# An encoder layer on one core: token tile 0 runs further ahead at the part boundaries, and the stationary operands move to the weights' byte

## The chip, the core and the metric

The kernel runs on one core of a Trainium2 chip. The metric is the device time of one execution in microseconds. Before the change it is 1952.46 us, the median of three runs (1952.25 to 1954.24).

## What is computed

One layer of an encoder on x of 256 tokens by 2,048 features in float32. It has three parts, each with an RMS norm before and after, and shift, scale and gate from a modulation vector (c times `w_ada`):

```python
h = modulate(rms_norm(x, ffn1_pre_g), sh1, sc1)
x = x + 0.5 * g1 * rms_norm((silu(h @ w_gate) * (h @ w_up)) @ w_down, ffn1_post_g)

h = modulate(rms_norm(x, mix_pre_g), sh2, sc2)
q, k, v, c_val, c_gate = split(h @ w_in)
attn = three dilated window attentions of rope(q), rope(k), v, combined
u = silu(layer_norm(depthwise_conv31(c_val * sigmoid(c_gate)) + conv_b))
merged = concat(rms_norm(attn), rms_norm(u)) @ w_out
x = x + g2 * rms_norm(merged, mix_post_g)

h = modulate(rms_norm(x, ffn2_pre_g), sh3, sc3)
x = x + 0.5 * g3 * rms_norm((silu(h @ w_gate) * (h @ w_up)) @ w_down, ffn2_post_g)
```

The inner width of both feed-forward parts is 5,632.

## The kernel before

**Products.** Each product of two float32 matrices is done as three TensorE products of a hi and a lo half. The 256 tokens are two token tiles, t0 and t1, of 128. Weights come in chunks of two k-tiles (2 x 128 rows by 512 columns, 512 KB): SyncE's queue loads a chunk into one of seven `raw` buffers, ScalarE casts it to `hi` (L290), and VectorE makes `lo` = raw - hi (L291); `hi` and `lo` have four buffers each (`HILO`). For each k-tile and token tile there are three matmuls: hi x xh (L316), lo x xh (L317), hi x xl (L318). The activations, 128 x 128, are the stationary operand; the weights, 128 x 512, move. There are 2,560 such triples, 7,680 matmuls.

`in_step` (L320) takes a list of chunks: it loads and casts them all, then runs all of t0's products on them, then all of t1's. `group` (L329) makes one step of each chunk, but joins the first `head` chunks, and the last `tail` chunks, into one step.

**Parts.** The first feed-forward part (ffn1) runs its first products in four stages over the features, while VectorE forms the modulation sums (L191) that the next stage needs. Then come mixing (w_in in column groups c0 to c3 for the convolution and q, k, v for the heads, then attention, convolution, and w_out as groups oa, ob, oc), and ffn2, again in stages. Work beside the products (modulation, attention, convolution) runs in lanes, which advance at a set rate at each `tick` of a chunk.

**Boundaries.** Between two parts the new x must be complete for a token tile before its norm. `next_norm` (L409) does it: `post_rstd` makes the post-norm's factor from the squares of f (POOL's power), `post_add` adds f to x in four pieces (VectorE, L405) with their squares (ScalarE, L339), and `pre_norm` scales x to `xn` (VectorE, L368), transposes it (TensorE, L371), applies the modulation (ScalarE, L376) and splits it to h (L357, L358), the stationary operand of the next part. So that t0 can go through this while TensorE still works for t1, the last group of ffn1 and the group oc3 have `TAIL` = 4 chunks in one step, all of t0 first; and the next part begins with `HEAD` = 4 chunks of c0, or g0 and u0 (four chunks) in `begin2` (L568), t0 first again.

**Addresses.** As built, the buffers of the weights (`raw`, `hi`, `lo`) begin at byte 64 of a 256-byte line. The slots of the activations (`slot`, L249: tags h and a) begin at byte 0, but for the slot `al5`, which follows a slot of `SLOT` = 1,144 elements and begins at byte 224. 128 of the 7,680 matmuls have their stationary operand there, all of them L318.

**The order of instructions** on each engine is set by a scheduler that works from dependencies and priorities, within the order of the program.

Of the kernel before, what the change touches and what calls it, by code (L numbers as in the profile page):

```python
# [34 lines left out]

HEAD = 4
TAIL = 4  # L40
# [20 lines left out]
def encoder_layer(ctx, tc, a, consts, out):  # L61
# [215 lines left out]
            return self.lo[k // 4][:, k % 4:k % 4 + n, :]  # L277


    def wchunk(w, r0, kt, cols, name):  # L280
# [12 lines left out]

    class Group:
# [6 lines left out]
            self.first, self.last, self.kx = first, last, kx  # L301
            self.chunks = -(-nk // CH)

        def load(self, c):
            kt = min(CH, self.nk - c * CH)
            return wchunk(self.w, (self.k0 + c * CH) * P, kt, self.cols, f"{self.name}_{c}")

        def products(self, c, t, hl):
            ts = slice(t * P, (t + 1) * P)
# [10 lines left out]
    def in_step(work):  # L320

        hls = [g.load(c) for g, c in work]
# [6 lines left out]
    def group(*args, head=0, tail=0, **kw):  # L329

        g = Group(*args, **kw)
        head = min(head, g.chunks - tail)
        mid = range(head, g.chunks - tail)
        for cs in (range(head), *([c] for c in mid), range(g.chunks - tail, g.chunks)):
            in_step([(g, c) for c in cs])
# [63 lines left out]
    def post_add(f, r, i, t):  # L399


        sx = small(f"sx{i}_{t}", 4)
        for db in range(4):
            xs = x[:, t, db * BLK:(db + 1) * BLK]
            nc.vector.scalar_tensor_tensor(xs, f[db][:, t, :], r, xs, op0=ALU.mult, op1=ALU.add)  # L405
            square_sum(xs, sx[:, db:db + 1], "jx")
        return rstd_parts(sx, D, f"r{i}_{t}", keep_in="rx")

    def next_norm(f, ssp, A, B, j1, i):  # L409

# [9 lines left out]
        return hT, rs  # L420
# [29 lines left out]
    def ffn_down(f, aT, wd, ba, bb, th, G, ssp, i):  # L450
        for db in range(4):
            pd = mm_ps(f"pd{i}_{th}_{db}")
            group(pd, aT, wd, ba * 4, (bb - ba) * 4, db * BLK, f"d{i}_{th}_{db}",
                  tail=TAIL if th == 1 and db == 3 else 0)
            for t in range(NT):
# [106 lines left out]
    rs = [rstd_parts(sx[t], D, f"r0_{t}", act=True, keep_in="rx") for t in range(NT)]  # L562
    for _ in first:
        pass
    hT = Parts("h1", "h", range(4))
    pre_norm(hT, rs, A1, B1, *STAGES1[0], "1_0")

    def begin2(open_group, run, order):  # L568

        gs, k1 = {}, STAGES2[0][1]  # L570
        for w, b in order[:2]:
            ps = mm_ps(f"p{w}2_{b}_0")
            gs[w, b] = open_group(w, b, 0, 0, k1, ps)
# [299 lines left out]
    drain(conv_entry)  # L873
    drain(mods)
    r2 = rc["conv"]
    for db in range(4):
        po = mm_ps(f"pc{db}")
        group(po, mT, w_out, 8, 8, db * BLK, f"oc{db}", kx=8, tail=TAIL if db == 3 else 0)
        for t in range(NT):
            nc.vector.scalar_tensor_tensor(f[db][:, t, :], po[t], r2[:, t:t + 1],  # L880
                                           f[db][:, t, :], op0=ALU.mult, op1=ALU.add)
            post_block(f, ssp, G2, t, db)


    hT, rs = next_norm(f, ssp, A3, B3, STAGES2[0][1], 3)
# [66 lines left out]
```

## Time and profile before

| | |
|---|---|
| median of three runs | 1952.46 us |
| profiled execution | 1953.91 us |
| its span | 1952.1 us |
| mean granted TensorE clock | 0.989 |
| TensorE (PE) busy | 1872.6 us, 96% |
| VectorE (DVE) busy | 1474.1 us, 76% |
| ScalarE (ACT) busy | 928.3 us, 48% |
| POOL busy | 66.0 us, 3% |
| moved by DMA | 496.29 MB, mean 254 GB/s |

The shares are means over a span with many stages; what bounds a stage has to be read in that stage. Busy times of matmuls are modelled at their ends, so the pace of TensorE is read from the starts of matmuls that follow each other. The page's part 4 follows the work that ended last back to the start.

### The profile page before, as it was taken

Reading aid. Unit: us, or ns where it says so; the run is one execution under the profiler, and the core shown is the slowest. Engines: PE = TensorE matmul, PEld = TensorE weight load, DVE = VectorE, ACT = ScalarE, POOL = GpSimd, SP = SyncE. Lnnn points to the kernel's source line nnn. Section 1 sums busy time; section 2 is a strip of 40 time slices with the busy share of each in tenths; the row PEclk is TensorE's granted clock in tenths of the full one; section 3 lists DMA queues with packets and bytes.
Section 4 is the critical chain, followed back from the end, with each engine's and each line's share of the span. In section 5 each row is a group of like instructions: output and inputs, shape, how many; then the busy total and the mean of one; then the engine's idle time right before and its main releaser. Section 6 shows DMA issues by size and latency. Waiting matters only on the chain.

```text
span 1952.1 us, 23783 instructions
## 1 busy us (share of the span) xinstructions
PE 1872.6 (96%) x8358; PEld 1527.1 (78%) x8358; DVE 1474.1 (76%) x1824; ACT 928.3 (48%) x1428; POOL 66.0 (3%) x99
## 2 busy tenths in 40 slices
PE   2999999999999999899999988999999999999997
PEld 1888877888888888688888776687888888888886
DVE  6789999787777776689997777897786556545455
ACT  3554355444444444644456655534444443444442
POOL 2000000000000000000100000000000000000000
PEclk9999999999999999899999999999999999999999
DMA  9989978999999898357555767897777777666653
GB/s 344 310 297 311 323 253 283 348 340 328 314 321 316 317 318 292 109 184 224 173 165 161 239 214 258 301 341 254 226 247 244 244 253 248 195 185 191 206 191 101
DMA packets 250392, 496.29 MB, mean 254 GB/s; under 512 B 17209, under 2 KB 42625, under 8 KB 250272
## 3 DMA queue, kind: packets, MB, share of 16 engines
q1 hardware_dynamic: 247888, 491.38, 76.1%
q0 software_dynamic: 2208, 3.32, 0.5%
q8 instruction: 65, 1.06, 0.2%
q14 instruction: 55, 0.45, 0.1%
q10 hardware_dynamic: 176, 0.07, 0.0%
HBM read 492.58 MB, written 2.12 MB: 253 GB/s over the span
## 4 chain that ended last, share of the span: by engine, by line
PE 88%; DVE 5%; DMA 3%; ACT 2%; issue 2%; POOL 0%; DVEq 0%; POOLq 0%; ACTq 0%; SPq 0%
PE pd_t L318 8%; PE pd_t L317 8%; PE pd_t L316 8%; PE pg_t L317 8%; PE pg_t L318 8%; PE pg_t L316 8%; PE pu_t L318 8%; PE pu_t L317 8%; PE pu_t L316 7%; PE pc_t L316 2%; PE pc_t L318 2%; PE pc_t L317 2%; DVE acc L191 2%; DMA ada<-in_w_ada 1%; PE pa L384 1%
## 5 line engine op out<-in xcount | busy, mean ns | idle before, releaser
L191 DVE SCALAR_TENSOR_TENSOR acc<-ada,cact,acc 128x512 f32<-128x512 f32 (+2 forms) x448 | 384.9, 897 | 12.8 <-DMA acc<-in_b_ada 8.4
L291 DVE TENSOR_TENSOR lo_d<-raw_d,hi_d 128x1024 fp32r<-128x1024 f32 x176 | 215.3, 1225 | 157.6 <-ACT hi_d L290 156.9
L290 ACT CAST hi_d<-raw_d 128x1024 fp32r<-128x1024 f32 x176 | 185.2, 1052 | 261.2 <-PE pd_t L318 181.5
L290 ACT CAST hi_g<-raw_g 128x1024 fp32r<-128x1024 f32 x176 | 185.0, 1052 | 247.2 <-PE pg_t L318 121.0
L291 DVE TENSOR_TENSOR lo_g<-raw_g,hi_g 128x1024 fp32r<-128x1024 f32 x176 | 214.4, 1222 | 105.0 <-ACT hi_g L290 104.8
L291 DVE TENSOR_TENSOR lo_u<-raw_u,hi_u 128x1024 fp32r<-128x1024 f32 x176 | 213.9, 1222 | 104.7 <-ACT hi_u L290 104.4
L290 ACT CAST hi_u<-raw_u 128x1024 fp32r<-128x1024 f32 x176 | 184.8, 1052 | 214.0 <-PE pu_t L318 94.5
L318 PE MATMUL pd_t<-hi_d,a_0l 128*128 128x512 f32 x384 | 151.2, 394 | 0.0
L317 PE MATMUL pd_t<-lo_d,a_0h 128*128 128x512 f32 x384 | 150.5, 392 | 0.0
L316 PE MATMUL pd_t<-hi_d,a_0h 128*128 128x512 f32 x384 | 150.4, 392 | 0.0
L316 PE MATMUL pg_t<-hi_g,h3h 128*128 128x512 f32 x352 | 140.4, 401 | 5.3 <-ACT hi_g L290 4.2
L316 PE MATMUL pu_t<-hi_u,h3h 128*128 128x512 f32 x352 | 139.8, 400 | 2.9 <-ACT hi_u L290 2.9
L317 PE MATMUL pu_t<-lo_u,h3h 128*128 128x512 f32 x352 | 140.0, 398 | 1.7 <-DVE lo_u L291 1.6
L317 PE MATMUL pg_t<-lo_g,h3h 128*128 128x512 f32 x352 | 139.4, 396 | 1.7 <-DVE lo_g L291 1.7
L316 PE MATMUL pg_t<-hi_g,h1h 128*128 128x512 f32 x352 | 139.4, 398 | 1.0 <-ACT hi_g L290 1.0
L318 PE MATMUL pu_t<-hi_u,h3l 128*128 128x512 f32 x352 | 139.7, 397 | 0.0
L317 PE MATMUL pg_t<-lo_g,h1h 128*128 128x512 f32 x352 | 138.7, 394 | 0.8 <-DVE lo_g L291 0.8
L318 PE MATMUL pg_t<-hi_g,h3l 128*128 128x512 f32 x352 | 139.3, 396 | 0.0
L316 PE MATMUL pu_t<-hi_u,h1h 128*128 128x512 f32 x352 | 138.8, 396 | 0.0
L318 PE MATMUL pu_t<-hi_u,h1l 128*128 128x512 f32 x352 | 138.6, 394 | 0.0
L318 PE MATMUL pg_t<-hi_g,h1l 128*128 128x512 f32 x352 | 138.6, 395 | 0.0
L317 PE MATMUL pu_t<-lo_u,h1h 128*128 128x512 f32 x352 | 137.8, 392 | 0.1
(259 smaller groups left out, 3572.1 us busy)
## 6 DMA issues: line engine op xcount, KB each, us to landing
ada<-in_w_ada SPq DMA_DIRECT2D x288, 512.0 KB, 5.3
raw_g<-in_ffn_w_gate SPq DMA_DIRECT2D x176, 512.0 KB, 4.7
raw_u<-in_ffn_w_up SPq DMA_DIRECT2D x176, 512.0 KB, 4.7
raw_d<-in_ffn_w_down SPq DMA_DIRECT2D x176, 512.0 KB, 5.7
raw_c<-in_w_in SPq DMA_DIRECT2D x64, 256.0 KB, 3.1
raw_q<-in_w_in SPq DMA_DIRECT2D x16, 512.0 KB, 4.4
raw_k<-in_w_in SPq DMA_DIRECT2D x16, 512.0 KB, 4.5
raw_v<-in_w_in SPq DMA_DIRECT2D x16, 512.0 KB, 4.2
```

The source lines that it names most:

```text
L191: tc.keep_in_program_order(nc.vector.scalar_tensor_tensor(acc, w[:, j, :], cact[:, j0 + j:j0 + j + 1], acc, op0=ALU.mult, op1=ALU.add))
L290: nc.scalar.copy(h, r)
L291: nc.vector.tensor_tensor(l, r, f32(h), op=ALU.subtract)
L316: nc.tensor.matmul(o, xh, h, start=self.first and k == 0, stop=False)
L317: nc.tensor.matmul(o, xh, l, start=False, stop=False)
L318: nc.tensor.matmul(o, xl, h, start=False, stop=self.last and k == self.nk - 1)
L384: nc.tensor.transpose(ps[:, jj * S + t * P:jj * S + (t + 1) * P], src[:, t, jj * P:(jj + 1) * P], ident)
```

## The change

**Boundaries.** The tail of each feed-forward part's last group is seven chunks (`TAIL1`), three of them with hi and lo in slots that are free by then (`TAIL_AT1`). oc2 and oc3 go together in one step of eight chunks (`TAIL_AT2`). All eight chunks of c0 have t0 first (`HEAD1`), and the first four are loaded and cast ahead of `next_norm`, into free slots of a (`HEAD_AT1`). ffn2 begins with g0, u0 and g1, six chunks, the first four again ahead (`HEAD_AT2`). `next_norm` takes the last group's evictions as a function: t0's first, t1's only behind t0's first transposes; t1's own norm comes after all of t0's. `begin2` reports six chunks instead of four, so the modulation's lane of that stage runs at 24/16 instead of 24/18 steps a chunk.

**Addresses.** `SLOT` is rounded up to 1,152 elements, so that no slot is off its line; and a tile `gap` of 64 bytes is put ahead of the first h tile. As built, all 7,680 matmuls then have both operands at byte 64.

The core of the diff:

```diff
-HEAD = 4
-TAIL = 4
+TAIL1 = 7
+TAIL_AT1 = (("hh2", "hl2"), ("hh3", "hl3"), ("gs", "ac"))
+HEAD1 = 8
+HEAD_AT1 = (("ah0", "al0"), ("ah1", "al1"), ("ah2", "al2"), ("ah3", "al3"))
+HEAD_AT2 = TAIL_AT2 = (("ah0", "ah1"), ("ah2", "ah3"), ("al2", "al3"), ("ah5", "al5"))
...
-SLOT = 4 * (S + 2 * PAD)
+SLOT = -(-4 * (S + 2 * PAD) // 64) * 64
...
-        hi = wpool.tile([P, CH, BLK], F32R, tag="hi", name=f"hi_{name}")
-        lo = wpool.tile([P, CH, BLK], F32R, tag="lo", name=f"lo_{name}")
+        if at is None:
+            hi = wpool.tile([P, CH, BLK], F32R, tag="hi", name=f"hi_{name}")
+            lo = wpool.tile([P, CH, BLK], F32R, tag="lo", name=f"lo_{name}")
+        else:
+            hi = slot(at[0], [P, CH, BLK], f"hi_{name}", F32R)
+            lo = slot(at[1], [P, CH, BLK], f"lo_{name}", F32R)
...
-    def next_norm(f, ssp, A, B, j1, i):
...
-        hT = Parts(f"h{i}", "h", range(4))
-        jh = min(HEAD * CH, j1)
+    def next_norm(hT, f, ssp, A, B, j1, i, evict):
...
+        evict(0)
         rs = [post_add(f, post_rstd(ssp, i, 0), i, 0)]
         pre_norm(hT, rs, A, B, 0, JF, i, 0, 1)
+        evict(1)
         rs.append(post_add(f, post_rstd(ssp, i, 1), i, 1))
-        pre_norm(hT, rs, A, B, JF, jh, i, 0, 1)
-        pre_norm(hT, rs, A, B, 0, jh, i, 1, 2)
-        pre_norm(hT, rs, A, B, jh, j1, i)
+        pre_norm(hT, rs, A, B, JF, j1, i, 0, 1)
+        pre_norm(hT, rs, A, B, 0, j1, i, 1, 2)
...
-                  tail=TAIL if th == 1 and db == 3 else 0)
+                  tail=TAIL1 if th == 1 and db == 3 else 0, places=TAIL_AT1)
...
+    nc.vector.memset(work.tile([P, 16], F32, name="gap"), 0.0)
     hT = Parts("h1", "h", range(4))
...
-        in_step([(g, c) for g in gs.values() for c in range(g.chunks)])
-        return {k: (g.ps, k1) for k, g in gs.items()}, k1
+        in_step(ahead2, hls=hls2 + load_all(ahead2[4:]))
+        return {k: (g.ps, STAGES2[0][1]) for k, g in heads2.items()}, len(ahead2)
...
+    c0 = Group(ps_c0, hT, a["w_in"], 0, NK, (3 * AW, 3 * AW + CW), "c0")
+    ahead = [(c0, c) for c in range(HEAD1)]
+    hls = load_all(ahead[:4], HEAD_AT1)
+    rs = next_norm(hT, f, ssp, A2, B2, NK, 2, evict)
+    in_step(ahead, hls=hls + load_all(ahead[4:]))
...
+    both = [conv_group(db) for db in (2, 3)]
+    in_step([(g, c) for g in both for c in range(g.chunks)], TAIL_AT2)
...
+    for w, b in (("g", 0), ("u", 0), ("g", 1)):
...
+    ahead2 = [(g, c) for g in heads2.values() for c in range(g.chunks)]
+    hls2 = load_all(ahead2[:4], HEAD_AT2)
+    rs = next_norm(hT, f, ssp, A3, B3, STAGES2[0][1], 3, evict)
```

How the order moves, at two places. First VectorE at the boundary from ffn1 to mixing, from t0's third addition to x (L405 before, L418 now) up to its first `xn`. L459 (now L472) evicts t1's last product, L390 multiplies it by the gate, `lo_c0_n` is a cast of chunk n of c0, `s_` are sums for the norms. Before:

```order
L405 SCALAR_TENSOR_TENSOR x_87<-f1_2_2759,pr2_0_6500,x_87 128x512
L459 TENSOR_TENSOR f1_3_2760<-pd1_1_3_t1_6302,f1_3_2760 128x512
L405 SCALAR_TENSOR_TENSOR x_87<-f1_3_2760,pr2_0_6500,x_87 128x512
L291 TENSOR_TENSOR lo_c0_1_6736<-raw_c0_1_6734,hi_c0_1_6735 128x1024
L390 TENSOR_TENSOR f1_3_2760<-f1_3_2760,G1l_5607 128x512
L291 TENSOR_TENSOR lo_c0_2_6743<-raw_c0_2_6741,hi_c0_2_6742 128x1024
L291 TENSOR_TENSOR lo_c0_3_6750<-raw_c0_3_6748,hi_c0_3_6749 128x1024
L350 TENSOR_REDUCE s_r2_0_6517<-sx2_0_6504 128x1
L350 TENSOR_REDUCE s_pr2_1_6542<-ssp1_2761 128x1
L351 TENSOR_SCALAR s_r2_0_6517<-s_r2_0_6517 128x1
L351 TENSOR_SCALAR s_pr2_1_6542<-s_pr2_1_6542 128x1
L368 TENSOR_SCALAR xn2_0_0_6523<-x_87,r2_0_6518 128x256
```

and now:

```order
L418 SCALAR_TENSOR_TENSOR x_87<-f1_2_2761,pr2_0_6528,x_87 128x512
L300 TENSOR_TENSOR lo_c0_2_6511<-raw_c0_2_6509,hi_c0_2_6510 128x1024
L418 SCALAR_TENSOR_TENSOR x_87<-f1_3_2762,pr2_0_6528,x_87 128x512
L300 TENSOR_TENSOR lo_c0_4_6739<-raw_c0_4_6737,hi_c0_4_6738 128x1024
L300 TENSOR_TENSOR lo_c0_3_6518<-raw_c0_3_6516,hi_c0_3_6517 128x1024
L472 TENSOR_TENSOR f1_3_2762<-pd1_1_3_t1_6304,f1_3_2762 128x512
L363 TENSOR_REDUCE s_r2_0_6545<-sx2_0_6532 128x1
L300 TENSOR_TENSOR lo_c0_5_6746<-raw_c0_5_6744,hi_c0_5_6745 128x1024
L364 TENSOR_SCALAR s_r2_0_6545<-s_r2_0_6545 128x1
L300 TENSOR_TENSOR lo_c0_6_6753<-raw_c0_6_6751,hi_c0_6_6752 128x1024
L381 TENSOR_SCALAR xn2_0_0_6551<-x_87,r2_0_6546 128x256
```

Casts of chunks 4 to 6 have come in, the multiply by the gate and t1's sums have moved behind `xn`.

Second, TensorE at the boundary from mixing to ffn2, where t1's first transposes (`pst3_0_1`, L371, now L384) stand among t0's products of the head. Before, in the head's third chunk (`pu2_0_0`):

```order
L317 MATMUL pu2_0_0_t0_9829<-lo_u2_0_0_0_0_9845,h3h0_9721 128x512
L318 MATMUL pu2_0_0_t0_9829<-hi_u2_0_0_0_0_9844,h3l0_9722 128x512
L316 MATMUL pu2_0_0_t0_9829<-hi_u2_0_0_0_0_9844,h3h0_9721 128x512
L317 MATMUL pu2_0_0_t0_9829<-lo_u2_0_0_0_0_9845,h3h0_9721 128x512
L371 MATMUL pst3_0_1_9795<-ident_75,xn3_0_1_9796 128x128 x2
L371 MATMUL pst3_2_1_9805<-ident_75,xn3_2_1_9806 128x128 x2
L318 MATMUL pu2_0_0_t0_9829<-hi_u2_0_0_0_0_9844,h3l0_9722 128x512
```

and now, in its sixth and last chunk (`pg2_1_0`):

```order
L325 MATMUL pg2_1_0_t0_9743<-hi_g2_1_0_0_0_9884,h3h0_9731 128x512
L326 MATMUL pg2_1_0_t0_9743<-lo_g2_1_0_0_0_9885,h3h0_9731 128x512
L327 MATMUL pg2_1_0_t0_9743<-hi_g2_1_0_0_0_9884,h3l0_9732 128x512
L325 MATMUL pg2_1_0_t0_9743<-hi_g2_1_0_0_1_9890,h3h0_9731 128x512
L384 MATMUL pst3_0_1_9851<-ident_75,xn3_0_1_9852 128x128 x2
L384 MATMUL pst3_2_1_9861<-ident_75,xn3_2_1_9862 128x128 x2
L326 MATMUL pg2_1_0_t0_9743<-lo_g2_1_0_0_1_9891,h3h0_9731 128x512
```

t1's transposes stand 14 of t0's products later (31 instead of 17 matmuls into the head).

## Rows read from the trace of the kernel before

**Rows 1.** The page, parts 1, 4 and 6, of the whole span.

```profile
PE 1872.6 (96%) x8358; PEld 1527.1 (78%) x8358; DVE 1474.1 (76%) x1824; ACT 928.3 (48%) x1428; POOL 66.0 (3%) x99
...
PE 88%; DVE 5%; DMA 3%; ACT 2%; issue 2%; POOL 0%; DVEq 0%; POOLq 0%; ACTq 0%; SPq 0%
...
raw_c<-in_w_in SPq DMA_DIRECT2D x64, 256.0 KB, 3.1
```

**Rows 2.** Stretches: us; busy PE, PEld, DVE, ACT, POOL; PE clock; DMA share; GB/s.

```profile
107.00:320.00 213.00, 210.81 (x956) 171.27 (x955) 202.58 (x257) 103.94 (x161) 4.80 (x7) 1.00 0.87 292
345.00:460.00 115.00, 115.00 (x511) 94.22 (x510) 89.57 (x76) 53.06 (x82) 2.87 (x4) 1.00 0.95 345
```

**Rows 3.** Waits of TensorE: waiting instruction, releaser, us in all, count, longest.

```profile
PE pst L371 <- DVE xn L368: 14.8, 2, 7.5
```

**Rows 4.** Timeline of VectorE, first boundary: start, us, instruction, [idle before, releaser].

```profile
793.98 0.69 DVE L459 TENSOR_TENSOR f<-pd_t,f 128x512 f32<-128x512 f32 x1 [3.23 <-PE pd_t L318]
...
805.44 0.15 DVE L350 TENSOR_REDUCE s_r<-sx 128x1 f32<-128x4 f32 x1
...
806.43 0.63 DVE L368 TENSOR_SCALAR xn<-x,r 128x256 f32<-128x256 f32 x2 [0.59 <-POOL r L352]
```

**Rows 5.** Timeline of TensorE at the same boundary.

```profile
799.10 0.40 PE L318 MATMUL pd_t<-hi_d,a_1l 128*128 128x512 f32 x1
806.84 1.12 PE L371 MATMUL pst<-ident,xn 128*128 128x128 f32 x4 [7.35 <-DVE xn L368]
```

**Rows 6.** The page, part 5: the casts (busy, mean ns, idle before).

```profile
L291 DVE TENSOR_TENSOR lo_d<-raw_d,hi_d 128x1024 fp32r<-128x1024 f32 x176 | 215.3, 1225 | 157.6 <-ACT hi_d L290 156.9
L290 ACT CAST hi_d<-raw_d 128x1024 fp32r<-128x1024 f32 x176 | 185.2, 1052 | 261.2 <-PE pd_t L318 181.5
```

**Rows 7.** Timelines of VectorE and TensorE at the second boundary.

```profile
1161.08 0.75 DVE L880 SCALAR_TENSOR_TENSOR fm<-pc_t,rcc,fm 128x512 f32<-128x512 f32 x1 [1.99 <-PE pc_t L318]
...
1173.62 0.63 DVE L368 TENSOR_SCALAR xn<-x,r 128x256 f32<-128x256 f32 x2 [0.59 <-POOL r L352]
...
1166.14 0.39 PE L318 MATMUL pc_t<-hi_oc,ml 128*128 128x512 f32 x1
1174.03 1.12 PE L371 MATMUL pst<-ident,xn 128*128 128x128 f32 x4 [7.50 <-DVE xn L368]
```

**Rows 8.** Stretches at the two boundaries, columns as in rows 2.

```profile
803.00:815.00 12.00, 7.04 (x20) 5.15 (x21) 8.00 (x21) 8.14 (x26) 1.76 (x3) 0.50 0.43 132
1163.00:1190.00 27.00, 18.39 (x73) 14.33 (x72) 19.17 (x38) 18.96 (x40) 3.09 (x4) 0.81 0.28 81
1190.00:1260.00 70.00, 63.57 (x266) 48.91 (x265) 59.80 (x93) 36.93 (x70) 3.88 (x6) 0.95 0.96 334
```

**Rows 9.** Timelines of VectorE and TensorE at the end.

```profile
1939.76 2.74 DVE L896 SCALAR_TENSOR_TENSOR f<-f,pr,x 128x512 f32<-128x512 f32 x4 [0.68 <-POOL pr L352]
1942.42 0.68 DVE L459 TENSOR_TENSOR f<-pd_t,f 128x512 f32<-128x512 f32 x1
...
1941.77 0.40 PE L318 MATMUL pd_t<-hi_d,a_1l 128*128 128x512 f32 x1
```

**Rows 10.** Timeline of TensorE: byte 224, byte 0, byte 0 early, one stationary operand.

```profile
712.25 0.40 PE L316 MATMUL pd_t<-hi_d,a_1h 128*128 128x512 f32 x1
...
715.75 0.40 PE L316 MATMUL pd_t<-hi_d,a_1h 128*128 128x512 f32 x1
...
716.45 0.39 PE L316 MATMUL pd_t<-hi_d,a_1h 128*128 128x512 f32 x1
...
725.37 0.39 PE L316 MATMUL pd_t<-hi_d,a_1h 128*128 128x512 f32 x1
...
101.60 0.40 PE L316 MATMUL pg_t<-hi_g,h1h 128*128 128x512 f32 x1
...
103.70 0.40 PE L316 MATMUL pg_t<-hi_g,h1h 128*128 128x512 f32 x1
...
1059.50 3.62 PE L761 MATMUL psmu<-co,ones 128*128 128x256 f32 x16
```

More of the change, by code (lines that the diff above doesn't have):

```diff
@@ L277, in l, with wchunk @@
             return self.lo[k // 4][:, k % 4:k % 4 + n, :]
-    def wchunk(w, r0, kt, cols, name):
+    def wchunk(w, r0, kt, cols, name, at=None):
         raw = wpool.tile([P, CH, BLK], F32, tag="raw", bufs=RAW, name=f"raw_{name}")
-        hi = wpool.tile([P, CH, BLK], F32R, tag="hi", name=f"hi_{name}")
-        lo = wpool.tile([P, CH, BLK], F32R, tag="lo", name=f"lo_{name}")
+        if at is None:
[4 more added lines that the diff above has]
+            lo = slot(at[1], [P, CH, BLK], f"lo_{name}", F32R)
         r, h, l = raw[:, :kt, :], hi[:, :kt, :], lo[:, :kt, :]
@@ L302, in __init__, with load @@
             self.chunks = -(-nk // CH)
-        def load(self, c):
+        def load(self, c, at=None):
             kt = min(CH, self.nk - c * CH)
-            return wchunk(self.w, (self.k0 + c * CH) * P, kt, self.cols, f"{self.name}_{c}")
+            return wchunk(self.w, (self.k0 + c * CH) * P, kt, self.cols, f"{self.name}_{c}", at)
         def products(self, c, t, hl):
@@ L318, in products, with load_all, in_step @@
                 nc.tensor.matmul(o, xl, h, start=False, stop=self.last and k == self.nk - 1)
-    def in_step(work):
-        hls = [g.load(c) for g, c in work]
+    def load_all(work, places=()):
+        return [g.load(c, places[n] if n < len(places) else None) for n, (g, c) in enumerate(work)]
+    def in_step(work, places=(), hls=None):
+        if hls is None:
+            hls = load_all(work, places)
         for t in range(NT):
@@ L327, in in_step, with group @@
             tick()
-    def group(*args, head=0, tail=0, **kw):
+    def group(*args, tail=0, places=(), **kw):
         g = Group(*args, **kw)
[L332 to L335, printed above, removed]
+        for c in range(g.chunks - tail):
+            in_step([(g, c)])
+        if tail:
+            in_step([(g, c) for c in range(g.chunks - tail, g.chunks)], places)
     def square_sum(src, dst, name):
@@ L407, in post_add @@
         return rstd_parts(sx, D, f"r{i}_{t}", keep_in="rx")
[L409 to L413 removed]
+    def next_norm(hT, f, ssp, A, B, j1, i, evict):
+        evict(0)
         rs = [post_add(f, post_rstd(ssp, i, 0), i, 0)]
         pre_norm(hT, rs, A, B, 0, JF, i, 0, 1)
+        evict(1)
         rs.append(post_add(f, post_rstd(ssp, i, 1), i, 1))
[L417 to L420 removed]
+        pre_norm(hT, rs, A, B, JF, j1, i, 0, 1)
+        pre_norm(hT, rs, A, B, 0, j1, i, 1, 2)
+        return rs
     def act_out(aT, i, gs, pu, name):
@@ L453, in ffn_down, with evict @@
             group(pd, aT, wd, ba * 4, (bb - ba) * 4, db * BLK, f"d{i}_{th}_{db}",
-                  tail=TAIL if th == 1 and db == 3 else 0)
-            for t in range(NT):
+                  tail=TAIL1 if th == 1 and db == 3 else 0, places=TAIL_AT1)
+            def evict(t, db=db, pd=pd):
                 if th == 0:
@@ L459, in ffn_down @@
                     nc.vector.tensor_tensor(f[db][:, t, :], pd[t], f[db][:, t, :], op=ALU.add)
-                if th == 1:
                     post_block(f, ssp, G, t, db)
+            if th == 1 and db == 3:
+                return evict
+            for t in range(NT):
+                evict(t)
     ROUNDS = ((0, 6, (0, 1, 2, 3, 4, 5)), (6, 11, (0, 1, 2, 3, 5)))
@@ L528, in ffn_rest @@
             G = gate() if th == 1 else None
-            ffn_down(f, aT, wd, ba, bb, th, G, ssp, i)
-        return f, ssp
+            evict = ffn_down(f, aT, wd, ba, bb, th, G, ssp, i)
+        return f, ssp, evict
     A1, B1 = affine_tiles(1)
@@ L568, in begin2 @@
     def begin2(open_group, run, order):
[L570 to L573, printed above, removed]
-        in_step([(g, c) for g in gs.values() for c in range(g.chunks)])
-        return {k: (g.ps, k1) for k, g in gs.items()}, k1
+        in_step(ahead2, hls=hls2 + load_all(ahead2[4:]))
+        return {k: (g.ps, STAGES2[0][1]) for k, g in heads2.items()}, len(ahead2)
     load_cols(("conv_b", "conv_ln_g", "conv_ln_b", "attn_out_g", "conv_out_g"), 1)
@@ L588, in encoder_layer @@
                    (later_mods(), LRATE))
-    f, ssp = ffn_rest(hT, aT, a["ffn1_w_gate"], a["ffn1_w_up"], a["ffn1_w_down"],
-                      lambda: gate_tile(g1, 1), 1)
+    f, ssp, evict = ffn_rest(hT, aT, a["ffn1_w_gate"], a["ffn1_w_up"], a["ffn1_w_down"],
+                             lambda: gate_tile(g1, 1), 1)
     drain_all()
-    hT, rs = next_norm(f, ssp, A2, B2, NK, 2)
+    QC = BLK // 2
+    hT = Parts("h2", "h", range(4))
+    ps_c0 = mm_ps("pc0")
+    c0 = Group(ps_c0, hT, a["w_in"], 0, NK, (3 * AW, 3 * AW + CW), "c0")
[3 more added lines that the diff above has]
+    in_step(ahead, hls=hls + load_all(ahead[4:]))
     w_in = a["w_in"]
@@ L616, in encoder_layer, with in_group @@
         nc.gpsimd.memset(u[:, :, PAD + S:], 0.0)
-    def in_group(o, name, head=0):
+    def in_group(o, name):
         ps = mm_ps(f"p{name}")
-        group(ps, hT, w_in, 0, NK, o, name, head=head)
+        group(ps, hT, w_in, 0, NK, o, name)
         return ps
@@ L830, in encoder_layer @@
     rc = {}
-    QC = BLK // 2
     conv_entry = None
     for g in range(CW // QC):
-        ps = in_group((3 * AW + g * QC, 3 * AW + CW + g * QC), f"c{g}", head=HEAD if g == 0 else 0)
+        ps = in_group((3 * AW + g * QC, 3 * AW + CW + g * QC), f"c{g}") if g else ps_c0
         gs = gs_tile(f"c{g}")
@@ L875, in encoder_layer, with conv_group, evict_c, evict @@
     r2 = rc["conv"]
-    for db in range(4):
-        po = mm_ps(f"pc{db}")
-        group(po, mT, w_out, 8, 8, db * BLK, f"oc{db}", kx=8, tail=TAIL if db == 3 else 0)
-        for t in range(NT):
[L880 to L885, printed above, removed]
+    pcs = [None] * 4
+    def conv_group(db):
+        pcs[db] = mm_ps(f"pc{db}")
+        return Group(pcs[db], mT, w_out, 8, 8, db * BLK, f"oc{db}", kx=8)
+    def evict_c(db, t):
+        nc.vector.scalar_tensor_tensor(f[db][:, t, :], pcs[db][t], r2[:, t:t + 1],
+                                       f[db][:, t, :], op0=ALU.mult, op1=ALU.add)
+        post_block(f, ssp, G2, t, db)
+    for db in range(2):
+        g = conv_group(db)
+        for c in range(g.chunks):
+            in_step([(g, c)])
+        for t in range(NT):
+            evict_c(db, t)
+    both = [conv_group(db) for db in (2, 3)]
+    in_step([(g, c) for g in both for c in range(g.chunks)], TAIL_AT2)
+    def evict(t):
+        for db in (2, 3):
+            evict_c(db, t)
+    hT = Parts("h3", "h", range(4))
+    heads2 = {}
+    for w, b in (("g", 0), ("u", 0), ("g", 1)):
+        heads2[w, b] = Group(mm_ps(f"p{w}2_{b}_0"), hT, a["ffn2_w_gate" if w == "g" else "ffn2_w_up"], 0,
+                             STAGES2[0][1], b * BLK, f"{w}2_{b}_0_0")
+    ahead2 = [(g, c) for g in heads2.values() for c in range(g.chunks)]
+    hls2 = load_all(ahead2[:4], HEAD_AT2)
+    rs = next_norm(hT, f, ssp, A3, B3, STAGES2[0][1], 3, evict)
     aT = ffn_start(hT, a["ffn2_w_gate"], a["ffn2_w_up"], 2, STAGES2, ffn2_mods,
@@ L888, in encoder_layer @@
                    (mod_gate(8, "ffn2_post_g", 0.5, g3), 0.3), begin2)
-    f, ssp = ffn_rest(hT, aT, a["ffn2_w_gate"], a["ffn2_w_up"], a["ffn2_w_down"],
-                      lambda: gate_tile(g3, 3), 2)
+    f, ssp, evict = ffn_rest(hT, aT, a["ffn2_w_gate"], a["ffn2_w_up"], a["ffn2_w_down"],
+                             lambda: gate_tile(g3, 3), 2)
     for t in range(NT):
+        evict(t)
         r = post_rstd(ssp, 4, t)
```

## The prediction

> **What bounds the kernel now.** I read the page's head first. TensorE is busy for 1872.6 of 1952.1 us and holds 88% of the chain that ended last [rows 1]; nothing else holds more than 5%. So the time is (number of matmuls) x (pace of one), plus the places where TensorE stands still. VectorE and DMA come into it where they run full: from 107 to 320 us VectorE is busy for 202.58 of 213 us, and from 345 to 460 us the DMA share is 0.95 [rows 2]. Next I read the waits of TensorE. Its largest single ones are two on the transposes `pst` of a new part, 14.8 us together [rows 3]: the two part boundaries. Last I read the starts of matmuls in steady stretches, since the change moves operands in SBUF.
>
> The profiled execution took 1953.91 us for a span of 1952.1; the median of the runs is 1952.46. I sum against 1953.9 and take 1.45 us off at the end. A change of 0.2%, 3.9 us, is about what can be told from none.
>
> **Boundary 1 (first FFN to mixing).** Token tile t0's last eviction is at 793.98 us and its first normalised block `xn` at 806.43 [rows 4]; the first transposes follow at 806.84, after 7.35 us of idle TensorE. The last of t1's products started at 799.10 [rows 5]. So t0's chain lasts 806.84 - 793.98 = 12.86 us, and t1's four chunks of work cover 24 matmuls x 0.229 us = 5.5 us of it (0.229 is a third of 0.686, below). The change keeps seven chunks for t1: three more, 3 x 6 x 0.229 = 4.1 us more cover. Against that stands what the scheduler puts between the links of the chain on VectorE. By the order of instructions there, three casts `lo` and two operations on `f` of t1 stood between the additions of x and `xn`; now five casts and one operation on `f` do. A cast costs 1.22 us on VectorE and 1.05 on ScalarE [rows 6], an operation on `f` 0.69 [rows 4]: the new mix is longer by 2 x 1.22 - 0.69 = 1.8 us if none of it falls into a wait, by nothing if all does. Gain 2.3 to 4.1; I take 3.2.
>
> **Boundary 2 (mixing to second FFN).** The same reading: t0's last eviction at 1161.08, `xn` at 1173.62, transposes at 1174.03 after 7.50 us of idle, t1's last product at 1166.14 [rows 7]. oc2 and oc3 now go together, so t1 covers eight chunks where it covered four: 4 x 6 x 0.229 = 5.5 us more. But t0's chain gets one more eviction (0.75 us, rows 7) with its multiply and up to two casts (2.4 us): up to 3.2 us longer. Gain 2.3 to 5.5; I take 3.2.
>
> Behind it the second FFN's stage 0 is fed badly: from 1163 to 1190 us the DMA share is 0.28, from 1190 to 1260 it is 0.96 with TensorE busy for 63.57 of 70 us [rows 8]. Casting four head chunks early, into free slots, frees four raw buffers, so four loads of 512 KB move into the quiet stretch: 2.1 MB at the 334 GB/s of that row is 6.3 us, and the idle to be won is 70 - 63.57 = 6.4. SyncE's queue issues these weights in the order of before, with the modulation's transfers one place later among them. Between 0 and 6.3 I take 2.2, a third, because two of the casts stand where t0's chain wants VectorE. The six-chunk head also puts t1's transposes behind fourteen more matmuls of t0, which is cover and not work. The higher rate of the modulation's lane in this stage (24/16 steps a chunk for 24/18) moves sums on VectorE and adds none. Boundary 2 in all: 5.4.
>
> Two edits I cost at nothing. The memset of the gap is one operation of 16 columns on VectorE, at most the 0.15 us that the smallest rows there take [rows 4], while the first weights still load. The load of the convolution's weights, which uses the slot `gs`, is issued on SyncE's queue some fifty transfers later, between the two halves of a chunk of c1, because `gs` now holds a chunk until t1's last product. What queues behind it is c1's weights; if they came late it would cost up to the 3.1 us that such a transfer takes to land [rows 1], and I take nothing, since eight chunks of c0 lie ahead of c1, 48 x 0.229 = 11 us of TensorE's work.
>
> The clock is a cost of both boundaries too. From 803 to 815 us its granted level is 0.50 [rows 8], so 1.2 GHz, after the standstill, and TensorE's 7 us there would be half as long at the full level. If the shorter standstill leaves the clock at the full level, up to 3.5 us more is won at each boundary; since a standstill of 3 us or more stays, I count nothing and keep the 7 us in the range.
>
> **The end.** t1's last eviction started at 1942.42, after its last product of 1941.77, behind t0's final operations [rows 9]. Seven chunks of cover let t0 finish earlier: 0.4 us at most, taken.
>
> **The addresses.** All 7,680 matmuls with 512 columns read weights at byte 64 of a 256-byte line and their stationary operand at byte 0, except 128 whose stationary part (the second of the odd-sized slots) lies at byte 224. The change rounds the slot and shifts every stationary tile by 64 bytes, so that all read (64, 64). The matmuls come in triples (hi, lo, hi). In a stretch with the third one's operand at byte 224, five triples take 715.75 - 712.25 = 3.50 us, 0.700 each; with it at byte 0, thirteen take 725.37 - 716.45 = 8.92 us, 0.686 each [rows 10]. Moving one of three stationary operands by 32 bytes thus costs 13 ns, on one matmul of 229. Rounding alone returns 126 x 13.3 ns = 1.7 us.
>
> What byte 64 costs no row shows, since no matmul of before reads it. The bounds: 16 back-to-back matmuls with one stationary operand take 3.62 us, so start to start (3.62 - 0.39) / 15 = 0.215 us [rows 10], which makes 0.648 for a triple, the least I see; and 0.700 above, which triples at byte 0 also show for a while (101.60 to 103.70 us, three triples in 2.10 us). The row with byte 0 against byte 224 says that the pace hangs on where the stationary operand lies, so I don't take 0.687 as fixed. I take half way from 0.687 down to the floor, 0.667: 20 ns x 2,560 triples = 51 us. Not all of it comes through: (956 + 511 + 266) of 8,358 matmuls, 21%, stand in stretches where VectorE or DMA is at 0.95 or more [rows 2, 8]. There I count about a quarter of it, so 0.85 in all: 43 us. The floor itself would give 39.3 ns x 2,560 x 0.85 = 85 us.
>
> The Trainium skill speaks against this term: "TensorE: Matmul & The Clock Gate", in "Part 2: What happens when you issue a matmul", says that weights and moving data are read through two independent ports, so that loading the next weights doesn't slow the running matmul. By that, the byte of the stationary operand is worth nothing and the sum is case F below. The 0.700 against 0.686 [rows 10] disagree with it, by 13 ns per matmul.
>
> **The sum.** 1953.9 - 3.2 - 5.4 - 0.4 - 1.7 = 1943.2 without the pace, 1941.8 on the median's scale; less 43: **1899 us**.
>
> **The rivals.**
> *G, my forecast:* the pace falls, to between 0.648 and 0.682 per triple. 1856 (floor) to 1932 (5 ns); 1899 half way. For it: 13 ns hang on 32 bytes, and 13 to 14 ns per matmul lie above the floor. Against it: the floor row loads the same operand each time, so part of the gap may be the change of operand itself. 0.48.
> *F, the addresses do nothing beyond byte 224:* only boundaries and 1.7 us, 1936 to 1947, 1942. For it: thirteen triples in a row at byte 0 keep 0.686, which looks like a fixed price. 0.29.
> *H, the other side:* two reads that begin at the same byte of a line get in each other's way, and every triple goes to 0.700. Place: all FFN stages. Price: 13.3 ns x 2,560 x 0.85 = 29 us: 1942 + 29 = 1971. It decides from the point where the triple passes 0.687 + 0.004 = 0.691, since 10.7 us at the boundaries pay for 4.2 ns. For it: bytes 0 and 64 differ now, and of the two distances shown one is dearer, so distance 0 may be too. Against it: byte 224 doesn't meet byte 64 and is dear all the same, so equal bytes aren't what makes that row dear. 0.16.
> *N, the boundaries backfire, the pace stays:* the head chunks' casts stand in t0's chain. Three lo x 1.22 and four hi x 1.05 make 7.9 us against 4.1 of cover at boundary 1, and as much at 2: 2 x 3.8 longer, and no gain in stage 0: 1952.5 + 7.6 - 1.7 - 0.4 = 1958, or 1956 when part of stage 0's gain is kept. 0.07.
> That the change doesn't do what it says is left out: the order shows both parts in place.
>
> **How the numbers follow.** Faster by over 0.2%: F nearly whole and G: 0.75 (0.48 and 0.27). Same: the edge of F and a mild H, 0.05. Slower: H and N with those edges off, 0.20. The likeliest case's own range is 1856 to 1932. The range has to hold 8 in 10, so it goes from G's floor with the clock's gain partly in (1853) over F and N to the milder half of H (1962), where two thirds of the triples' 13 ns come through.
>
> **What would show it.** Triples start to start in steady stretches of the changed kernel: 0.667 (G), 0.687 (F, N), 0.700 (H). TensorE's idle ahead of the first transposes: about 4.2 us at each boundary in place of 7.35 and 7.50; over 8 means N. DMA share from the boundary's quiet stretch above 0.28, and TensorE's idle in stage 0 down by 2 us. With byte 224 gone no stretch should differ from the others by the operand's slot. The forecast is wrong if the triple's pace is not under 0.682, or if VectorE's or DMA's share caps the stages so that the time falls by less than half of what the pace gives.

## The result and the profile after

The changed kernel takes 1926.11 us (median of four runs, 1925.60 to 1927.09) against 1952.54 in the same comparison: a ratio of 0.9863, interval 0.9846 to 0.9881. It is 26.4 us faster. The forecast of 1899 gave twice that gain; the time lies within the range of 1853 to 1962 and within case G's own (1856 to 1932).

The head of the page and the chain, to be held against [rows 1]:

```profile
span 1923.8 us, 23785 instructions
...
PE 1850.4 (96%) x8358; PEld 1522.1 (79%) x8358; DVE 1472.8 (77%) x1829; ACT 930.7 (48%) x1440; POOL 68.8 (4%) x99
...
PE 85%; DVE 6%; DMA 3%; ACT 3%; issue 2%; POOL 0%; DVEq 0%; POOLq 0%; ACTq 0%; SPq 0%
```

TensorE has the same 8,358 instructions and 22.2 us less busy time, so most of the 28.3 us by which the span is shorter (1952.1 to 1923.8) is pace, of the matmuls or of the clock, and not idle time. A trace is one execution; the medians of the runs differ by 26.4 us. The waits of TensorE, against [rows 3] (waiting instruction, releaser, us in all, count, longest):

```profile
PE pst L384 <- DVE xn L381: 9.4, 2, 4.7
...
PE pu_t L326 <- DVE lo_u L300: 4.9, 2, 4.4
```

The two boundaries idle for 9.4 us instead of 14.8. A wait for `lo_u`, at most 0.5 us long before, is now 4.4. The pace in a steady stretch of ffn1's last groups, against [rows 10] (timeline of TensorE: start, us, instruction):

```profile
700.14 0.39 PE L325 MATMUL pd_t<-hi_d,a_1h 128*128 128x512 f32 x1
...
711.02 0.39 PE L325 MATMUL pd_t<-hi_d,a_1h 128*128 128x512 f32 x1
```

Sixteen triples in 10.88 us: 0.680 us each, 0.227 a matmul. Before it was 0.686; 0.667 had been forecast. Of the 2,355 triples that another triple follows directly, 2,080 take 0.680; the stretches at 0.700 are gone.

The first boundary, timelines of VectorE and TensorE of the changed kernel, against [rows 4, 5], and the second on TensorE, against [rows 7]:

```profile
782.16 0.69 DVE L472 TENSOR_TENSOR f<-pd_t,f 128x512 f32<-128x512 f32 x1 [7.21 <-PE pd_t L327]
...
789.48 0.75 DVE L418 SCALAR_TENSOR_TENSOR x<-f,pr,x 128x512 f32<-128x512 f32 x1
...
795.93 0.61 DVE L381 TENSOR_SCALAR xn<-x,r 128x256 f32<-128x256 f32 x2 [0.44 <-POOL r L365]
...
791.25 0.39 PE L327 MATMUL pd_t<-hi_d,a_1l 128*128 128x512 f32 x1
796.34 1.11 PE L384 MATMUL pst<-ident,xn 128*128 128x128 f32 x4 [4.70 <-DVE xn L381]
...
1158.92 1.12 PE L384 MATMUL pst<-ident,xn 128*128 128x128 f32 x4 [4.70 <-DVE xn L381]
```

t0's chain from its last eviction to the transposes was 12.86 us and is 796.34 - 782.16 = 14.18: 1.3 us longer, inside the 0 to 1.8 of the prediction. t1's cover grew from 5.5 to 9.5 us, about the 4.1 forecast, so idle fell by 2.65 us (7.35 to 4.70), and at the second boundary by 2.80 (7.50 to 4.70).

### The profile page after: what moved, and what is told of

It reads as the page before. It is cut to its first block, busy times and chain, and to the rows that moved or that the text cites. A ratio compares the mean times of both kernels' runs of the same rounds, so it can differ in the third digit from the quotient of the medians.

```text
span 1923.8 us, 23785 instructions
## 1 busy us (share of the span) xinstructions
PE 1850.4 (96%) x8358; PEld 1522.1 (79%) x8358; DVE 1472.8 (77%) x1829; ACT 930.7 (48%) x1440; POOL 68.8 (4%) x99
## 4 chain that ended last, share of the span: by engine, by line
PE 85%; DVE 6%; DMA 3%; ACT 3%; issue 2%; POOL 0%; DVEq 0%; POOLq 0%; ACTq 0%; SPq 0%
PE pd_t L327 8%; PE pd_t L325 8%; PE pd_t L326 8%; PE pg_t L326 8%; PE pg_t L327 8%; PE pg_t L325 8%; PE pu_t L327 7%; PE pu_t L326 7%; PE pu_t L325 7%; DVE acc L195 2%; PE pc_t L327 2%; PE pc_t L326 2%; PE pc_t L325 2%; DMA raw_g<-in_ffn_w_gate 1%; DMA ada<-in_w_ada 1%
```

## Experiments

Theory A: the address of the stationary operand, relative to the weights', sets the pace; the boundaries give the rest. Theory B: the new order gives it all. All experiments start from the changed kernel unless the label says otherwise.

**e1: the addresses alone, in the kernel before.**

```diff
-SLOT = 4 * (S + 2 * PAD)
+SLOT = -(-4 * (S + 2 * PAD) // 64) * 64
...
+    nc.vector.memset(work.tile([P, 16], F32, name="gap"), 0.0)
     hT = Parts("h1", "h", range(4))
```

> The kernel before with the rounded slot and the gap alone, so that all 7,680 matmuls read (64, 64). Theory A (the addresses set the pace: a triple goes from 0.687 us to the 0.680 seen after the change, and the triples at 0.700 go there too): 6.7 ns x 2,371 + 20 ns x 189 = 19.6 us less, 1933 us, triples at 0.680. Theory B (the new order of the work made the pace, the addresses only take byte 224 away): 1.7 us less, 1951 us, triples at 0.687.

1938.54 us against 1950.64 beside it: 0.9935, interval 0.9920 to 0.9950; the span went from 1952.1 to 1936.3. The triples, on TensorE's timeline:

```profile
706.23 0.39 PE L316 MATMUL pd_t<-hi_d,a_1h 128*128 128x512 f32 x1
...
708.95 0.39 PE L316 MATMUL pd_t<-hi_d,a_1h 128*128 128x512 f32 x1
```

Four in 2.72 us, 0.680. So the pace is the addresses' doing: A. But the 19.6 us expected came only to 12.1 (medians) or 15.8 (spans of one execution each).

**e2: the changed kernel with the stationary operands back at byte 0.**

```diff
-    nc.vector.memset(work.tile([P, 16], F32, name="gap"), 0.0)
```

> The changed kernel without the gap: weights at byte 64, stationary operands at byte 0, no operand at byte 224. Theory A: triples at 0.687, 6.7 ns x 2,560 = 17 us more than the changed kernel, 1943 to 1944 us; what is left against before, 9 us, is the boundaries' with 1.7 us of byte 224. Theory B: 1926 us, triples at 0.680.

1939.33 us, ratio 0.9946 (0.9930 to 0.9963), span 1937.0. The triples are back:

```profile
701.64 0.39 PE L325 MATMUL pd_t<-hi_d,a_1h 128*128 128x512 f32 x1
...
715.37 0.39 PE L325 MATMUL pd_t<-hi_d,a_1h 128*128 128x512 f32 x1
```

Twenty in 13.73 us, 0.6865. Against the changed kernel that is 13.2 us, and 15.0 against e4 below, which has equal bytes and ran on the same chip as e2; the expectation had 17. By spans the two halves of the change give 15.8 (e1) and 15.1 (e2), 1.7 of which (byte 224) is in both: 29.2, near the 28.3 of the whole. By the medians of that chip they give 12.1 and 11.3, so 21.7 together, where e4, as good as the whole change, gives 26.3. The intervals of e1 and e2 are some 3 us either way, so whether the halves simply add up isn't settled.

**e3, e4, e8, e11, e12: which address is good.** The same kernel with other gaps, and in e4 with the weights moved too:

```diff
-    nc.vector.memset(work.tile([P, 16], F32, name="gap"), 0.0)
+    nc.vector.memset(work.tile([P, 32], F32, name="gap"), 0.0)
...
+    nc.vector.memset(keep.tile([P, 48], F32, name="pad"), 0.0)
```

(32 columns is e3's gap of 128 bytes; the `pad` is e4's alone, with the gap of 16. e8, e11 and e12 have gaps of 48, 24 and 8 columns.)

> The changed kernel with a gap of 128 bytes: weights at 64, stationary operands at 128; the 216 matmuls of the chunks in free slots read (128, 128). Theory S (the pace is best where both operands begin at the same byte of the line): triples at 0.687 or more, 1943 us or more, the 216 at 0.227 each. Theory T (byte 0 is dear for a stationary operand and others are not): triples at 0.680, 1926 us.

> The changed kernel with 192 bytes put ahead of the weights, so that both operands of all 7,680 matmuls begin at byte 0. Theory S: triples at 0.680, 1926 us. Theory T: triples at 0.687, 1943 us.

> The changed kernel with a gap of 192 bytes: weights at 64, stationary operands at 192, 128 bytes on. If only the same byte is best and the price grows with the distance: triples above the 0.700 of 64 bytes on. If the line is read in two halves, so that 128 bytes on counts as the same place: 0.680. If any other byte costs alike: 0.687 to 0.700.

> The changed kernel with a gap of 96 bytes: weights at 64, stationary operands at 96, 32 bytes on. If the price comes with any distance: triples at 0.687 to 0.700. If it comes only once the distance is 64 or more: 0.680.

> The changed kernel with a gap of 32 bytes: weights at 64, stationary operands at 32, 32 bytes back. If the distance counts by its size, as in the run with 32 bytes on; if the direction counts as well (64 bytes back cost 7 ns a triple, 64 on cost 20), less than that, 0.680 to 0.687.

| weights at | stationary at | distance | typical triple, us | time, us |
|---|---|---|---|---|
| 64 | 64 (the change) | 0 | 0.680 | 1926.11 |
| 0 | 0 (e4) | 0 | 0.680 | 1924.33 |
| 64 | 0 (e2) | -64 | 0.687 | 1939.33 |
| 64 | 128 (e3) | +64 | 0.700 | 1967.77 |
| 64 | 192 (e8) | +128 | 0.690 to 0.706 | 1963.18 |
| 64 | 96 (e11) | +32 | 0.698 to 0.702 | 1966.05 |
| 64 | 32 (e12) | -32 | 0.698 to 0.703 | 1964.72 |

(e8, e11 and e12 are one run each.) One row pair each of e3 and e4, timeline of TensorE:

```profile
705.20 0.40 PE L325 MATMUL pd_t<-hi_d,a_1h 128*128 128x512 f32 x1
...
710.80 0.39 PE L325 MATMUL pd_t<-hi_d,a_1h 128*128 128x512 f32 x1
```

```profile
705.79 0.39 PE L326 MATMUL pd_t<-hi_d,a_1h 128*128 128x512 f32 x1
...
708.51 0.39 PE L326 MATMUL pd_t<-hi_d,a_1h 128*128 128x512 f32 x1
```

Eight triples in 5.60 us, 0.700; four in 2.72, 0.680. Theory S holds: the pace is best where both operands begin at the same byte, wherever that is, and T falls with e3 and e4. Of the five other distances tried only -64, the kernel before's, is anything less than the full 0.700 (or close to it, +128). The 216 matmuls of the chunks in free slots show the same inside one run, since both of their operands lie in slots: in e2, e12, e11, e3 and e8 they read equal bytes, 0, 32, 96, 128 and 192. Of the 56 such triples that can be followed in each, 29, 33, 39, 38 and 42 take 0.680 and nearly all the rest 0.684 to 0.704, in runs whose typical triple takes 0.687 to 0.706. Had the direction counted, e12 would have cost less than e11; it doesn't. In all the pairs called equal the two addresses are also a multiple of 512 bytes apart, so the runs don't tell whether 256 bytes is the length that counts.

Why -64 is cheaper than the others is open, and at that distance the addresses don't settle the pace alone: 79 triples in a row in the kernel before, the first at 51.2 us and the last at 105.8, take 0.700, and the same triples at the very same addresses take 0.687 in e2. What holds such a stretch at one pace or the other isn't shown.

**e5: the feed-forward tails at four chunks.**

```diff
-TAIL1 = 7
+TAIL1 = 4
...
-                  tail=TAIL1 if th == 1 and db == 3 else 0, places=TAIL_AT1)
+                  tail=TAIL1 if th == 1 and db == 3 else 0, places=())
```

> The changed kernel with the feed-forward tails back at four chunks, none in free slots. By the prediction's step for boundary 1, t1 covers 24 x 0.227 = 5.4 us of a chain of 12.9 to 14.2 us, so TensorE idles 7.4 to 8.8 us ahead of the first transposes in place of 4.70, and the time is 2.7 to 4.1 us more, 1929 to 1930 us. Rival (the chain is as long as whatever covers it): the idle time stays near 4.7 and the time at 1926.

1929.30 us, 3.2 more than the changed kernel, and on TensorE's timeline:

```profile
798.45 1.11 PE L384 MATMUL pst<-ident,xn 128*128 128x128 f32 x4 [7.74 <-DVE xn L381]
```

7.74 us of idle, the step's 7.4 to 8.8. The cover by t1's chunks is real, at the size forecast. It is the idle time that shows it: the medians were not taken side by side, and the changed kernel's own differ by 1.6 us from one comparison to the next (1926.11, and 1927.71 in e10).

**e6: four chunks in ffn2's head.**

```diff
-    for w, b in (("g", 0), ("u", 0), ("g", 1)):
+    for w, b in (("g", 0), ("u", 0)):
```

> The changed kernel with g0 and u0 alone in the second feed-forward part's head (four chunks; the modulation's lane back at 24/18). Theory P (the longer head and the faster lane removed the 3.70 us wait and the low clock at the end of stage 1, which gave 6 us): they come back, 1931 to 1932 us. Theory Q (that wait went with the weights' pace or by chance of the transfers): 1926 to 1927 us, no wait above 2.5 us there.

1924.19 us, and the longest wait at the end of stage 1 is 2.06. P falls: neither g1 in the head nor the lane's rate removed the wait of before. (Of Q the wait came true; its time was 1926 to 1927.) The 1.9 us below the changed kernel aren't settled by this: stage 0 alone differs by that much between two executions of the changed kernel (83.5 and, in e10, 85.4 us from the first transposes to stage 1).

**e7: the casts of the heads' later chunks behind t0's chain.**

```diff
+    def load_late(work):
...
-        nc.scalar.copy(h, r)
-        nc.vector.tensor_tensor(l, r, f32(h), op=ALU.subtract)
+        with behind("act"):
+            nc.scalar.copy(h, r)
+        with behind("dve"):
+            nc.vector.tensor_tensor(l, r, f32(h), op=ALU.subtract)
...
+    in_step(ahead, hls=hls + load_late(ahead[4:]))
```

(`behind` queues what it holds after t0's last square on ScalarE, or its first `xn` on VectorE; the same for g1's chunks.)

> The changed kernel with the casts of the heads' later chunks (c0's chunks 4 to 7, g1's two) queued behind t0's first xn on VectorE and behind t0's last square on ScalarE. Theory C (these casts lengthen t0's chain): at boundary 1 three lo casts of 1.22 us and one eviction leave it, so the idle time goes from 4.70 to 1 to 2.5 us, at boundary 2 from 4.70 to 2 to 3.5 us, and the time falls by 3 to 6 us with the clock's share, 1920 to 1923 us. Theory D (the links of the chain themselves take the time, or VectorE must do the casts a little later on the path anyway): idle time over 4 us or a new wait for lo of the same size, 1926 us.

1923.77 us. The chain and its end at the first boundary, timelines of VectorE and TensorE:

```profile
790.05 0.75 DVE L434 SCALAR_TENSOR_TENSOR x<-f,pr,x 128x512 f32<-128x512 f32 x1
790.98 1.23 DVE L314 TENSOR_TENSOR lo_c<-raw_c,hi_c 128x1024 fp32r<-128x1024 f32 x1 [0.18 <-ACT hi_c L312]
...
793.12 0.61 DVE L395 TENSOR_SCALAR xn<-x,r 128x256 f32<-128x256 f32 x2 [0.66 <-POOL r L379]
...
793.52 0.70 PE L400 MATMUL pst<-ident,xn 128*128 128x128 f32 x4 [1.32 <-DVE xn L395]
...
1152.97 0.70 PE L400 MATMUL pst<-ident,xn 128*128 128x128 f32 x4 [1.88 <-DVE xn L395]
```

From the last addition of x to `xn` it is 793.12 - 790.05 = 3.07 us; in the changed kernel it was 795.93 - 789.48 = 6.45. Idle falls from 4.70 to 1.32 and 1.88, as C says (at the second boundary by a little more). The time doesn't follow as far: 1923.77 is outside C's 1920 to 1923, and its ratio of 0.9858 (0.9844 to 0.9873) can't be told from the changed kernel's 0.9863. Of the 3.4 us at the first boundary 2.4 reach q0. At the second boundary ffn2 starts 6.0 us earlier than in the changed kernel (transposes at 1152.97 against 1158.92), but stage 1 only 2.4 us earlier. The 4.4 us wait for `lo_u` stands in both and isn't what takes it back; new waits for t1's own norm do. TensorE's timeline, then its waits:

```profile
1168.18 0.70 PE L400 MATMUL pst<-ident,xn 128*128 128x128 f32 x4 [1.64 <-DVE xn L395]
...
PE pg_t L339 <- ACT h3h L384: 3.0, 2, 1.8
```

In the changed kernel t1's transposes wait for nothing (they start at 1171.06), and the waits for `h3h` are 1.3 us in all. Once t0's chain is shorter, t0's head products end before t1's chain does. e7 moves the casts of both engines at once; which of them stood in the way isn't separated.

**e9 and e10: both edits, and the changed kernel beside it.** The edits are those of e6 and e7.

> The changed kernel with the late casts and the second feed-forward part's head of four chunks together. If the 3 us of the one and the 2 us of the other lie in different stretches (the first boundary and stage 0) they add up: 1921 to 1922 us, about 4 us under the changed kernel on the same chip. If both are won from the same loads of stage 0, no more than 2 to 3 us: 1923 to 1924 us.

> The changed kernel once more, beside the runs of this call: 1924 to 1927 us, to compare e9 with on one chip.

1921.82 us (0.9842, interval 0.9828 to 0.9857) against 1927.71 for the changed kernel on the same chip (0.9874, interval 0.9858 to 0.9891; a little above the 1924 to 1927 expected): 5.9 us less. e9 beats both kernels. With four chunks in the head there is no later chunk whose cast could be moved, so e7's edit acts at the first boundary alone: q0 starts 3.0 us earlier than in e10, while the idle time at the second boundary is 4.22 us.

## Where the 28 us came from

The start of the first matmul of some groups in three traces, the kernel before, e1 (addresses alone) and the changed kernel, in us. Each is one execution. The medians of e1 and of the kernel before on one chip differ by 12.1 us where these spans differ by 15.8, so differences of a microsecond or two mean little:

| first matmul of | before | e1 | changed |
|---|---|---|---|
| ffn1's last group (d3) | 771.8 | 764.9 | 764.3 |
| q0, after c0 to c3 | 907.4 | 898.8 | 895.0 |
| the second boundary's transposes | 1174.0 | 1165.3 | 1158.9 |
| ffn2, stage 1 | 1260.0 | 1249.9 | 1242.4 |
| ffn2, stage 2 | 1369.1 | 1358.7 | 1345.8 |
| ffn2's last group (d3) | 1914.4 | 1898.9 | 1886.1 |
| end of the span | 1952.1 | 1936.3 | 1923.8 |

Column e1 against before is the addresses: 6.9 us up to ffn1's last group, 1.7 and 0.1 through the mixing part, 1.7 in ffn2's stages 0 and 1 and 5.4 behind them. Column changed against e1 is the order: 0.6 us in ffn1, then 3.2 over the first boundary and up to q0, 2.6 up to the second one's transposes, 1.1 in stage 0, **5.4 in stage 1**, and behind that it is 0.4 us longer.

Stage 1's 5.4 us was not on the list. At its end the kernel before waits for a cast that is queued behind modulation sums on VectorE, and the clock falls; the changed kernel waits there too, less long. The sums on VectorE, the cast on ScalarE, the wait on TensorE's timeline and the clock (stretch: us; busy PE, PEld, DVE, ACT, POOL; PE clock; DMA share; GB/s), all of the kernel before:

```profile
1332.21 6.42 DVE L191 SCALAR_TENSOR_TENSOR acc<-ada,cact,acc 128x256 f32<-128x256 f32 x16
...
1340.97 1.04 ACT L290 CAST hi_g<-raw_g 128x1024 fp32r<-128x1024 f32 x1 [6.13 <-DVE lo_u L291]
...
1342.07 0.79 PE L316 MATMUL pg_t<-hi_g,h3h 128*128 128x512 f32 x1 [3.70 <-ACT hi_g L290]
...
1342.00:1350.00 8.00, 7.93 (x23) 6.29 (x24) 4.29 (x11) 2.11 (x3) 0.00 (x0) 0.63 0.87 288
```

The wait and the clock in the changed kernel:

```profile
1327.60 0.50 PE L326 MATMUL pg_t<-lo_g,h3h 128*128 128x512 f32 x1 [2.03 <-DVE lo_g L300]
...
1325.00:1336.00 11.00, 8.97 (x42) 7.13 (x41) 11.00 (x18) 3.88 (x5) 0.00 (x0) 1.00 0.95 324
```

After 3.70 us of standstill the granted clock was 0.63 over the next 8 us, and 23 matmuls filled them; after 2.03 it stayed at 1.00. e1 still has the old wait (4.05 us), and e2, with the new order and the old bytes, has the short stage: from stage 1 to stage 2 it is 109.1 us before, 108.8 in e1, 104.1 in e2 and 103.4 in the changed kernel. So the order moved it. Which of its edits did was not found: e6 rules out two, and e5, with 103.5, the longer tail.

At the boundaries the clock falls in both kernels, for less long now. Before, then changed:

```profile
806.80:815.00 8.20, 7.04 (x20) 5.15 (x21) 4.79 (x13) 6.52 (x20) 0.81 (x2) 0.50 0.32 102
```

```profile
796.30:801.70 5.40, 4.89 (x14) 3.39 (x15) 4.97 (x13) 4.49 (x14) 0.58 (x1) 0.50 0.69 215
801.70:806.00 4.30, 4.30 (x22) 3.46 (x22) 3.63 (x11) 3.58 (x11) 0.58 (x1) 0.98 0.25 80
```

A shorter standstill alone didn't spare the boundary the low clock. In e7 the standstill was 1.32 us. TensorE then was busy for 1.64 of 2.5 us at a granted clock of 0.97, and from 796 us on it was at 0.50 again, busy throughout:

```profile
796.00:799.00 3.00, 3.00 (x9) 2.15 (x9) 2.56 (x9) 3.00 (x8) 0.58 (x1) 0.50 0.54 173
```

## Why the prediction was right or wrong

**What bounds the kernel, right.** TensorE's pace and its standstills carry the whole gain; no engine's work was taken away. One reading was wrong without harm: the two waits on `pst` aren't TensorE's largest single ones. Those are 20.4 and 7.9 us, in the first 36 us of the kernel, and the change leaves them as they were (20.5 and 8.1).

**Boundary 1, right.** Idle fell by 2.65 us where 3.2 was taken from 2.3 to 4.1, with the chain 1.3 us longer. e5 shows the cover, e7 the casts in the chain, each alone. The whole boundary up to q0, clock included, gave the 3.2 (table). c1 starts 5.7 us earlier than in e1, but 1.9 of that is no gain: the eight transposes of the convolution's weights, which ran during c0 before (826.1 to 834.3 us), now run when c1 has begun (826.1 to 829.8 us), and at some 0.23 us each they make about 1.9. They are done later and not twice, so the prediction's nothing for that edit holds.

**Boundary 2, right in the boundary, wrong behind it.** 2.80 us of idle for the 3.2 taken. In stage 0 the loads did move into the quiet stretch, as the stretches that match those of [rows 8] show:

```profile
1147.00:1174.00 27.00, 21.02 (x80) 16.29 (x80) 24.09 (x42) 18.13 (x40) 4.21 (x4) 0.81 0.68 204
1174.00:1244.00 70.00, 63.90 (x280) 51.19 (x279) 56.63 (x91) 39.52 (x74) 3.89 (x6) 0.95 0.87 295
```

The DMA share there is 0.68 for 0.28, but TensorE is busy for 63.90 of 70 us where it was 63.57: the idle time that was to fall by 2 us fell by 0.3 (by the waits of stage 0 behind its first transposes, from 7.5 to 7.4). A wait of 4.4 us for a cast stands late in the stage now, in place of several short ones. So earlier loads didn't give TensorE its idle time back. The stage is 1.1 us shorter than in e1 in this execution and 0.8 longer in e10, so none of the 2.2 is shown.

**The end, wrong.** Nothing came for the 0.4 us: from the last group's start to the end it is 37.7 us against 37.4 in e1.

**Stage 1, not seen.** 5.4 us came from a wait that the prediction didn't price, for which the order was not read that far. That the order's part comes out near its forecast is luck in this respect: the sum had 9.0 us for the boundaries and the end, and 6.5 came where it was priced (3.2, 2.6, 1.1, less 0.4).

**The addresses: the step that failed.** "I take half way from 0.687 down to the floor, 0.667" was the mis-sized term. The triple went to 0.680: 7 ns for the 20 taken. And of 6.7 ns x 2,371 + 20 ns x 189 = 19.6 us, 15.8 came through in e1's span, 0.81 of it, and 12.1 in its median, 0.62; 0.85 had been taken. So the term was 12 to 16 us with byte 224, where 43 + 1.7 had been put. What misled was the floor: 0.215 us is the start to start of matmuls with 256 columns of plain float32, where the weights are 512 columns of fp32r, and nothing in the rows tied it to these. 0.680 a triple is the least that any of the address pairs shows, and within such a triple the second matmul, whose stationary operand is the first one's, takes 0.227 as the others do, so the change of operand isn't the 12 ns in between; what makes the other row faster isn't shown. (By its own sums the floor is 3 x 0.215 = 0.646, and case G's upper end 1931, not 1932; neither matters.) The contrast there was, byte 0 against byte 224, told rightly that the place counts, but not that 64 would be better than 0: of the five places tried besides 0, with the weights at 64, four are dearer (32, 96, 128, 192). That the pace fell and didn't rise was in part luck. The size of that contrast, 13 ns on one matmul, is the difference between a distance of -64 and one of no special kind (the last four rows of the table), and a single such operand in a triple already costs those 13 ns; it isn't a step on a scale that could go on downwards as far.

**The rivals.** H, that equal bytes collide, is turned round by e4: equal bytes are best at either place. N falls: the casts do stand in the chain (e7), but cost less than the cover gives (e5). F describes e2, at 1939.33 inside its 1936 to 1947. Its rule, the Trainium skill's in "TensorE: Matmul & The Clock Gate", "Part 2: What happens when you issue a matmul", is that loading weights takes nothing from the running matmul's reads. As the prediction read it, the stationary operand's byte would be worth nothing; the table disagrees, since that byte alone moves the pace from 0.680 to 0.700 a triple. By what path it does so isn't shown.

## What to carry to other kernels

Where a kernel is bound by back-to-back matmuls with a new stationary operand each, look at the byte at which both operands begin in a 256-byte line, and place them alike: 32 bytes apart cost 3% of each matmul here, and a tile of 64 bytes and a rounded slot put it right. Take a floor only from a row with the same shape and type; when the only contrast is between two values, what a third gives is a range and not its middle. At a boundary between dependent parts count the cover in matmuls of the other tile, then read the engines' orders for casts that the scheduler has put between the links; and when t0's chain gets shorter, look at t1's next: in e7 its waits gave 3.6 us of an earlier start back.

## What was not expected of the hardware

The pace goes with the distance between the operands' first bytes and not with either: (0, 0) and (64, 64) both give 0.680 us a triple, 32 bytes either way 0.700, and 64 bytes are 0.687 one way and 0.700 the other. At -64 it can also stay at 0.700 for 79 triples in a row, at addresses that give 0.687 in another kernel. And a standstill of 3.70 us was followed by a granted clock of 0.63 over 8 us in one stage of the kernel before, where one of 2.03 us at the same place of the changed kernel left it at 1.00; yet in e7 one of 1.32 us, followed by transposes and a second wait, was followed by 0.50.
